# Second layer: 128 instead of 256 columns for the context's tiles in three projection blocks

## The chip, the cores and the metric

One Trainium2 chip, and of it one core. The metric is the time of one execution on the device in microseconds, as the median of several runs. The core's engines run side by side and meet by semaphores: TensorE multiplies (PE in the profile, and PEld for its loading of weights), VectorE (DVE) and ScalarE (ACT) work element by element, GpSimd (POOL) too, and SyncE (SP) starts most of the transfers from HBM.

## The reference, cut to what matters

Two layers of a block that mixes tokens and then runs a feed-forward part. There are 256 tokens of context and 256 of the sequence proper (x). Of the context the second layer, the last, needs only what the sequence reads from it: keys, values and the state of two scans. Its queries and its output gates have no reader.

```python
pc = split_cols(hc @ w_in + b_in)        # context, 256 tokens
px = split_cols(hx @ w_in + b_in)        # sequence, 256 tokens
mc, mx = mlstm_mixer(pc[0:6], px[0:6], ...)
gc, gx = hgrn2_mixer(pc[6:10], px[6:10], ...)
ac, ax = diff_mixer(pc[10:13], px[10:13], ...)
# with_ctx is False in the last layer: mc, gc and ac are not formed
# columns of w_in, in order: mLSTM q 384, k 384, v 384, output gate 384, i 8, f 8,
#   HGRN2 q 512, f 1024, v 256, gate 256, attention q 384, k 384, v 384
```

## The kernel before

All 512 tokens stand as four tiles of 128: tiles 0 and 1 are the context, 2 and 3 the sequence. The normalised input is kept transposed in `hT`, as two F32R parts: a rounded part, and what the rounding left. A weight block is fetched as F32 (`wraw`), ScalarE casts it to F32R (`whi`, line 297) and VectorE forms the rest (`wlo`, line 298). Each product is then made of three F32R matmuls: both parts of the activations by `whi` (`upper`), and the rounded part by `wlo` (`lower`). All of them are issued by one helper, `mm` in line 302, so that line stands for every projection of the kernel. No F32R matmul of the kernel has a moving operand of under 256 columns: they have 256, 400 or 512.

`gemm_tm` is the projection with tokens on the partitions of the output. The stationary operand (lhsT) is a 128x128 piece of `hT`, and the moving operand is the weight block, 256 columns wide in the blocks here. A block comes in two halves of the contraction with four pieces of 128 rows each. In each half, for each of the tiles in turn, `upper` issues eight matmuls; then `lower` issues four for each tile. Each matmul has a stationary piece of its own. Tiles 0 and 1 share a PSUM bank, and so do tiles 2 and 3; at the end `evac` takes each bank out with the bias added.

In the second layer (`l == 1`, `full` false) `qt` is (2, 3): blocks that hold queries or gates alone are computed for the sequence's two tiles only. The queries of the attention and of the mLSTM, however, are 384 columns wide, and so are the values. Cut into blocks of 256 columns, the middle one of each three is mixed:

- attention, `O_DAQ + 256`: columns 0 to 127 are queries, 128 to 255 are keys (into `qk`, by `add_bias`, line 913)
- mLSTM values and gates, `O_MLV + 256`: columns 0 to 127 are values, 128 to 255 are output gates (by `ev_vo`, lines 1069 to 1077)
- mLSTM queries and keys, `O_MLQ + 256`: columns 0 to 127 are queries, 128 to 255 are keys (into `mqk`, by `add_bias`)

These three blocks are computed with all 256 columns for all four tiles.

What runs where, and in what order, is not written out by hand. The program is written in order, each engine gets one fixed list of instructions, and the list is made by a planner that works with its own estimates of durations and with priorities: work marked `high_priority` (the casts in `wload`) goes ahead, and independent work is put where an engine would wait. So the blocks of the projections are found as filling between the steps of other stages: the attention's middle block between the steps of the HGRN2 scan (`hg_mix`, lines 798 to 880), the values' middle block between the steps of the attention (`da_tile`, lines 982 to 1003), and the mLSTM queries and keys one after another in a dense run. Other names in the rows are `Qd` and `Ck` (operands of the HGRN2 scan), `aT` and `Vda` (weights and values of the attention, plain F32) and `ls`, `lf` and `ct` (small plain-F32 products of the mLSTM's gates, lines 721 and 723, with 32 and 16 columns moving).

Of the kernel before, what the change touches and what calls it, by code (L numbers as in the profile page):

```python
# [15 lines left out]
ALU = mybir.AluOpType  # L16
# [15 lines left out]
O_MLQ, O_MLV, O_MLO, O_MLI = 0, 768, 1152, 1536  # L32
O_HGQ, O_HGF, O_HGV = 1552, 2064, 3088
O_DAQ, O_DAV = 3600, 4368
# [67 lines left out]
def dit_block(ctx: ExitStack, tc: tile.TileContext, x, c, ctx_in, c_ctx, w_ada, b_ada, g_pre_mix,  # L102
# [3 lines left out]
    V, S, G, PE, SY = nc.vector, nc.scalar, nc.gpsimd, nc.tensor, nc.sync  # L106
# [18 lines left out]
    def nm(s):  # L125
        uid[0] += 1
        return f"{s}_{uid[0]}"

    def pst(shape, mm=False):
        if mm:  # L130
            return psm.tile(shape, F32, tag="mm", name=nm("mm"))
        return psx.tile(shape, F32, tag="mx", name=nm("mx"))
# [126 lines left out]
    def ada_step():  # L259
        pace[0] += 1  # L260
        if pending and pace[0] % pace[1] == 0:
            try:
                next(pending[0])
            except StopIteration:
                pending.pop(0)
                ada_step_now()
# [14 lines left out]
    def wload(srcs, hold=None, eng=None):  # L281

        tot = sum(src.shape[1] for src in srcs)
        dims = [P, 4, 256] if tot <= 256 else [P, 2, 512]
        raw = wp.tile(dims, F32, tag="wraw", name=nm("wraw"), bufs=3)
        if hold is not None:
            hi, lo = hold
        else:
            hi = wp.tile(dims, F32R, tag="whi", name=nm("whi"), bufs=2)
            lo = wp.tile(dims, F32R, tag="wlo", name=nm("wlo"), bufs=2)  # L290
        n = 0
        for src in srcs:
            nk, w = src.shape[0] // P, src.shape[1]
            SY.dma_start(out=raw[:, :nk, n:n + w], in_=src.rearrange("(k p) n -> p k n", p=P))
            n += w
        with tc.high_priority(offset=AHEAD):
            S.copy(hi[:, :nk, :n], raw[:, :nk, :n])  # L297
            (eng or V).tensor_tensor(lo[:, :nk, :n], raw[:, :nk, :n], hi[:, :nk, :n], op=ALU.subtract)  # L298
        return hi, lo

    def mm(ps, lhs, rhs, first, last):
        PE.matmul(ps, lhsT=lhs, rhs=rhs, start=first, stop=last, skip_group_check=True)  # L302

    def upper(ps, blk, act, t, first):
        hi, _, ks = blk
        for kk, k in enumerate(ks):
            mm(ps, act(0, k, t), hi[:, kk], first and kk == 0, False)
            mm(ps, act(1, k, t), hi[:, kk], False, False)

    def lower(ps, blk, act, t, last):  # L310
        _, lo, ks = blk
        for kk, k in enumerate(ks):
            mm(ps, act(0, k, t), lo[:, kk], False, last and k == ks[-1])

    def blocks_of(srcs, holds=None):

        k0 = 0
        for si, pieces in enumerate(srcs):
            nk, n = pieces[0].shape[0] // P, sum(p.shape[-1] for p in pieces)
            hi, lo = wload(pieces, holds and holds[si])  # L320
            yield hi[:, :, :n], lo[:, :, :n], range(k0, k0 + nk)
            k0 += nk

    def gemm_tm(srcs, act, tiles, evac, pre=None):

        n = sum(p.shape[-1] for p in srcs[0])
        tiles = list(tiles)
        wide = n > 256  # L330
        bank = lambda t: t if wide else t // 2
        banks = {b: pst([P, 512] if wide else [P, 2, 256], mm=True) for b in sorted({bank(t) for t in tiles})}
        dst = lambda t: banks[t][:, :n] if wide else banks[bank(t)][:, t % 2, :n]
        new = lambda t: wide or t - 1 not in tiles or t % 2 == 0
        for si, blk in enumerate(blocks_of(srcs)):
            end = si == len(srcs) - 1
            if pre is not None and end:
                pre()
            if wide and end:
                for t in tiles:  # L340
                    upper(dst(t), blk, act, t, si == 0)
                    lower(dst(t), blk, act, t, True)
                    evac([t], dst(t))
            else:

                for t in tiles:
                    upper(dst(t), blk, act, t, si == 0 and new(t))
                for t in tiles:
                    lower(dst(t), blk, act, t, end)
            ada_step()  # L350
        if not wide:
            for tb, b in banks.items():
                tt = [t for t in tiles if bank(t) == tb]
                evac(tt, b[:, tt[0] % 2:tt[-1] % 2 + 1, :n])
# [39 lines left out]
    def w_src(w, c0, n):  # L394
        return [[w[kh * 512:(kh + 1) * 512, c0:c0 + n]] for kh in range(2)]
# [26 lines left out]
    hact = lambda i, k, t: hT[i][:, k, t * P:(t + 1) * P]  # L422
# [186 lines left out]
    for l in range(DEPTH):  # L609
        full = l == 0  # L610
        lam_init = 0.8 - 0.6 * math.exp(-0.3 * l)
        qt = (0, 1, 2, 3) if full else (2, 3)
# [79 lines left out]
        if l == 0:  # L692
            b0_load()
            for t in range(4):
                ev_first([t], acc0[t])
        else:
            srcs = first_src(l)
            gemm_tm(srcs, hact, (0, 1), ev_first, pre=b0_load)
            late_norm()
            gemm_tm(srcs, hact, (2, 3), ev_first)  # L700
# [194 lines left out]
        def ev_g(tt, ps):  # L895

            for i, t in enumerate(tt):
# [4 lines left out]
                V.tensor_mul(g_, g_, sg)  # L902
        hg_proj(1)
        gemm_tm(w_src(w_in[l], O_HGV + 256, 256), hact, qt, ev_g, pre=bg.load)
        lockstep(hg_mix(2), hg_mix(3))
        hg_out(2)
# [2 lines left out]
        hst.close()  # L909


        def add_bias(dst, w, nb, bb):
            return lambda tt, ps: V.tensor_tensor(dst[:, tt[0]:tt[-1] + 1, w:w + nb], ps[:, :, :nb],
                                                  bb.over(0, nb, len(tt)), op=ALU.add)

        qk = stg.tile([P, 4, 768], F32, tag="qk", name=nm("qk"))
        for i in range(3):
            bb = Bias([b_in[l, O_DAQ + i * 256:O_DAQ + (i + 1) * 256]])
            gemm_tm(w_src(w_in[l], O_DAQ + i * 256, 256), hact, qt if i == 0 else range(4), add_bias(qk, i * 256, 256, bb), pre=bb.load)
        bb = Bias([b_in[l, O_DAV:O_DAV + 256]])  # L920
        gemm_tm(w_src(w_in[l], O_DAV, 256), hact, range(4), add_bias(Vda, 0, 256, bb), pre=bb.load)

        wst = ExitStack()
# [135 lines left out]
        for i in range(3):  # L1059
            bb = Bias([b_in[l, O_MLV + i * 256:O_MLV + (i + 1) * 256]])  # L1060

            def ev_vo(tt, ps, i=i, bb=bb):
                c_ = 0
                while c_ < 256:
                    a = i * 256 + c_
                    if a < 384:
                        h, o = divmod(a, ML_D)
                        w = min(ML_D - o, 256 - c_, 384 - a)
                        V.tensor_tensor(Vml[:, tt[0]:tt[-1] + 1, h, o:o + w], ps[:, :, c_:c_ + w],
                                        bb.over(c_, c_ + w, len(tt)), op=ALU.add)  # L1070
                    else:
                        w = 256 - c_
                        for j, t in enumerate(tt):
                            if t in qt:
                                yv = Y[t][:, a - 384:a - 384 + w]
                                V.tensor_add(yv, ps[:, j, c_:], bb[:, c_:])
                                S.activation(yv, yv, AF.Sigmoid)
                    c_ += w
            gemm_tm(w_src(w_in[l], O_MLV + i * 256, 256), hact, range(4) if i < 2 else qt, ev_vo, pre=bb.load)
        mqk = stg.tile([P, 4, 768], F32, tag="qk", name=nm("mqk"))  # L1080
        for i in range(3):
            bb = Bias([b_in[l, O_MLQ + i * 256:O_MLQ + (i + 1) * 256]])
            gemm_tm(w_src(w_in[l], O_MLQ + i * 256, 256), hact, qt if i == 0 else range(4), add_bias(mqk, i * 256, 256, bb), pre=bb.load)

        dst_.close()
        gst = ExitStack()
# [165 lines left out]
        with tc.tile_pool(name=f"ff{l}", bufs=1, reuse_waits="tile") as ff:  # L1252
# [17 lines left out]
            for gi, (c0, ncb) in enumerate(groups):  # L1270
# [8 lines left out]
                for cp, a, b in blocks:  # L1279
                    cc_ = (c0 + 2 * cp) * P  # L1280
                    if cp not in GT:
                        GT[cp] = alloc()
                    n = b - a
# [91 lines left out]
```

## Time and profile before

| | us |
|---|---|
| median of 3 runs | 1347.56 |
| lowest and highest | 1346.56 and 1349.05 |
| the profiled execution, by the same clock | 1347.59 |
| its span, first to last instruction | 1345.9 |
| TensorE matmul busy | 1284.2 (95%) |
| TensorE weight load busy | 1094.6 (81%) |
| VectorE, ScalarE, GpSimd busy | 898.6, 624.9, 202.3 |
| mean granted TensorE clock, share of full speed | 0.985 |

The profile is one execution. A busy time is the union of an engine's instructions, and a matmul's length in it contains the way through the array, which the next matmul overlaps; so the pace of a run of matmuls is read from start to start and not from the length of one. A form such as `128*128 128x256` gives the stationary operand's size and then the moving operand's, and the names `mm<-whi,hT` put the moving operand before the stationary one. A row of the timeline joins successive instructions of one kind: start, time from the first start to the last end, and their count. A plain-F32 matmul stands in the records as two matmuls with two weight loads; an F32R matmul as one.

### The profile page before, as it was taken

To read this page: it belongs to the slowest core of one execution; us is meant where nothing else is said; L and a number is where in the kernel's file an instruction comes from. 1 tells how busy PE (TensorE), PEld (TensorE's weight loads), DVE (VectorE), ACT (ScalarE), POOL (GpSimd) and SP (SyncE) were. 2 spreads that over 40 slices of the span, in tenths; PEclk is the share of its full clock that TensorE was granted. 3 is DMA by queue.
4 is the path that set the end of the run, shared out by engine and by line. 5 is a ranking of instruction groups with operands and counts; after the bars stand their busy time and mean duration, and the time that the engine had idled before them with its cause. 6 is when DMAs were issued, how large, how long until landed. Compare 5 with 4: busy or idle time off the path is not lost.

```text
span 1345.9 us, 23128 instructions
## 1 busy us (share of the span) xinstructions
PE 1284.2 (95%) x9022; PEld 1094.6 (81%) x9022; DVE 898.6 (67%) x1564; ACT 624.9 (46%) x1188; POOL 202.3 (15%) x304
## 2 busy tenths in 40 slices
PE   7998999999989899999999999899999998999997
PEld 5785889778888798778887888778897998788886
DVE  4899998554688998476336348566855456666666
ACT  3436352578354653212221236546536724554543
POOL 3133202111142300001000003133111202000001
PEclk9999999999989999999999999899999999899999
DMA  9772526132244677477335235532331313456563
GB/s 290 227 221 75 164 64 201 41 114 72 95 141 142 192 253 229 141 255 243 116 100 178 94 111 151 148 95 63 104 95 51 122 47 109 142 188 188 188 188 125
DMA packets 158443, 194.05 MB, mean 144 GB/s; under 512 B 10524, under 2 KB 132806, under 8 KB 158334
## 3 DMA queue, kind: packets, MB, share of 16 engines
q1 hardware_dynamic: 156910, 188.89, 44.9%
q0 software_dynamic: 1424, 3.68, 1.0%
q8 instruction: 71, 1.16, 0.3%
q14 instruction: 38, 0.31, 0.1%
HBM read 191.47 MB, written 1.08 MB: 143 GB/s over the span
## 4 chain that ended last, share of the span: by engine, by line
PE 76%; DVE 10%; ACT 5%; issue 4%; DMA 3%; POOL 3%; SPq 0%; DVEq 0%; POOLq 0%; ACTq 0%
PE mm L302 62%; DMA araw<-in_w_ada_dram 2%; PE mx L1126 2%; DVE wlo L298 2%; PE mx L982 2%; PE mx L1003 1%; DVE acc L228 1%; PE mm L1114 1%; ACT whi L297 1%; POOL rstd L416 1%; PE mx L997 1%; PE mm L164 1%; DVE accq L228 1%; PE mx L880 1%; PE ada L233 1%
## 5 line engine op out<-in xcount | busy, mean ns | idle before, releaser
L297 ACT CAST whi<-wraw 128x1024 fp32r<-128x1024 f32 (+1 forms) x247 | 256.4, 1039 | 415.7 <-PE mm L302 365.2
L298 DVE TENSOR_TENSOR wlo<-wraw,whi 128x1024 fp32r<-128x1024 f32 (+1 forms) x243 | 295.8, 1218 | 193.0 <-PE mm L302 94.4
L302 PE MATMUL mm<-hT,whi 128*128 128x512 f32 (+1 forms) x1568 | 352.0, 372 | 4.4 <-ACT hT L465 2.1
L302 PEld LDWEIGHTS mm<-hT,whi 128*128 128x128 f32 x1568 | 270.8, 189 | 55.7 <-issue 4.0
L302 PE MATMUL mm<-whi,hT 128*128 128x256 f32 (+1 forms) x1792 | 264.3, 293 | 3.1 <-ACT hT L1157 1.4
L302 PEld LDWEIGHTS mm<-whi,hT 128*128 128x128 f32 x1792 | 234.0, 192 | 19.2 <-issue 8.4
L302 PE MATMUL mm<-hT,wlo 128*128 128x256 f32 (+1 forms) x960 | 185.0, 334 | 0.0
L302 PEld LDWEIGHTS mm<-hT,wlo 128*128 128x128 f32 x960 | 152.9, 190 | 21.1 <-issue 0.4
L302 PE MATMUL mm<-wlo,hT 128*128 128x256 f32 (+1 forms) x896 | 140.8, 292 | 0.0
L302 PE MATMUL mm<-whi,GT 128*128 128x512 f32 x504 | 129.5, 397 | 0.0
L302 PEld LDWEIGHTS mm<-wlo,hT 128*128 128x128 f32 x896 | 119.1, 191 | 10.9 <-issue 10.4
L302 PEld LDWEIGHTS mm<-whi,GT 128*128 128x128 f32 x504 | 93.7, 188 | 24.5 <-ACT whi L297 1.6
L228 DVE SCALAR_TENSOR_TENSOR accq<-araw,csil,accq 128x1024 f32<-128x1024 f32 x63 | 81.2, 1295 | 29.8 <-DMA araw<-in_w_ada_dram 29.7
L302 PE MATMUL mm<-wlo,GT 128*128 128x512 f32 x252 | 70.0, 396 | 0.0
L228 DVE SCALAR_TENSOR_TENSOR acc<-araw,csil,acc 128x1024 f32<-128x1024 f32 x49 | 62.8, 1306 | 4.6 <-DMA araw<-in_w_ada_dram 4.4
L302 PEld LDWEIGHTS mm<-wlo,GT 128*128 128x128 f32 x252 | 47.3, 188 | 11.3
L415 POOL TENSOR_SCALAR rstd<-hss 128x1 f32<-128x1 f32 (+2 forms) x44 | 18.8, 427 | 241.7 <-ACT hsq L656 159.9
L1327 POOL TENSOR_TENSOR Z<-Z,gg 128x512 f32<-128x512 f32 x6 | 9.4, 1572 | 234.1 <-ACT sqz L1326 234.1
L988 ACT ACTIVATE e<-mx,damx 128x512 f32<-128x512 f32 (+1 forms) x48 | 29.3, 618 | 26.3 <-DVE damx L985 26.3
L811 ACT COPY Ck<-Kh 128x512 f32<-128x512 f32 (+1 forms) x56 | 28.8, 525 | 25.7 <-DVE Kh L836 18.9
L416 POOL TENSOR_TENSOR rstd<-rstd,mhalf 128x1 f32<-128x1 f32 (+2 forms) x58 | 40.0, 690 | 4.7
L984 DVE TENSOR_REDUCE damx<-mx 128x1 f32<-128x512 f32 (+1 forms) x48 | 28.3, 598 | 18.0 <-PE mx L982 17.1
(283 smaller groups left out, 1499.9 us busy)
## 6 DMA issues: line engine op xcount, KB each, us to landing
araw<-in_w_ada_dram SPq DMA_DIRECT2D x80, 512.0 KB
wraw<-in_w_in_dram SPq DMA_DIRECT2D x68, 512.0 KB
wraw<-in_w_ffn_down_dram SPq DMA_DIRECT2D x50, 512.0 KB
wraw<-in_w_ffn_gate_dram SPq DMA_DIRECT2D x48, 512.0 KB
wraw<-in_w_ffn_up_dram SPq DMA_DIRECT2D x48, 512.0 KB
wraw<-in_w_out_dram SPq DMA_DIRECT2D x24, 512.0 KB
aw<-in_w_ada_dram SPq DMA_DIRECT2D x16, 512.0 KB
wraw<-in_w_in_dram SPq DMA_DIRECT2D x12, 256.0 KB
```

What stands on the lines that cost most here:

```text
L164: PE.matmul(acc0[3][:, :P], lhsT=ident, rhs=ident, start=True, stop=True, skip_group_check=True)
L228: V.scalar_tensor_tensor(out=a, in0=raw, scalar=csil[:, k, r:r + 1], in1=a, op0=ALU.mult, op1=ALU.add)
L297: S.copy(hi[:, :nk, :n], raw[:, :nk, :n])
L298: (eng or V).tensor_tensor(lo[:, :nk, :n], raw[:, :nk, :n], hi[:, :nk, :n], op=ALU.subtract)
L302: PE.matmul(ps, lhsT=lhs, rhs=rhs, start=first, stop=last, skip_group_check=True)
L415: G.tensor_scalar(o[:, :width], ss, 1.0 / n, EPS, ALU.mult, ALU.add)
L416: G.tensor_tensor(o[:, :width], o[:, :width], mhalf[:, :width], op=ALU.pow)
L811: S.copy(C[:, q0:].rearrange("p (a b i) -> p b a i", b=2, i=m), vap(K_, 2 * m * pq0, [[512 + m, 2], [2 * m, np_], [1, m]]))
L982: PE.matmul(pv[j], lhsT=qkT[0][64 * j:64 * j + DA_D, h, t * P:(t + 1) * P], rhs=qkT[1][64 * j:64 * j + DA_D, h, :nk], start=True, stop=True)
L984: V.reduce_max(mx[:, j:j + 1], pv[j], axis=AX.X)
L988: S.activation(e[:, j, :nk], pv[j], AF.Exp, bias=mx[:, 2 + j:3 + j], scale=sc, accum_out=mx[:, 4 + j:5 + j])
L1126: PE.matmul(po[:, i, d_, :], lhsT=W[d_, s_][0][:, t * P - W[d_, s_][2]:(t + 1) * P - W[d_, s_][2]], rhs=Vml[:, s_, h, :], start=n_ == 0, s ...
```

## The change

`gemm_tm` gets an argument `ctx_cols`. Where it is given, the matmuls of tiles 0 and 1 read only those columns of the weight block and write only those of the bank; tiles 2 and 3 are as before. `need` gives the pair of columns for the middle block (`i == 1`) in the second layer, and nothing elsewhere. `add_bias` evacuates only these columns of tiles 0 and 1. `ev_vo` is unchanged: it took no gates from tiles 0 and 1 of the second layer before either. The count of matmuls, the weight loads, the transfers and the casts are unchanged.

```diff
-    def gemm_tm(srcs, act, tiles, evac, pre=None):
+    def gemm_tm(srcs, act, tiles, evac, pre=None, ctx_cols=None):
...
+        part = lambda t: slice(*ctx_cols) if ctx_cols and t < 2 else slice(0, n)
...
+            of = lambda t: (blk[0][:, :, part(t)], blk[1][:, :, part(t)], blk[2])
...
                 for t in tiles:
-                    upper(dst(t), blk, act, t, si == 0 and new(t))
+                    upper(dst(t)[:, part(t)], of(t), act, t, si == 0 and new(t))
                 for t in tiles:
-                    lower(dst(t), blk, act, t, end)
+                    lower(dst(t)[:, part(t)], of(t), act, t, end)
...
-        def add_bias(dst, w, nb, bb):
-            return lambda tt, ps: V.tensor_tensor(dst[:, tt[0]:tt[-1] + 1, w:w + nb], ps[:, :, :nb],
-                                                  bb.over(0, nb, len(tt)), op=ALU.add)
+        need = lambda i, a, b: (a, b) if i == 1 and not full else None
+
+        def add_bias(dst, w, nb, bb, cc_=None):
+            def ev(tt, ps):
+                a, b = cc_ if cc_ and tt[0] < 2 else (0, nb)
+                V.tensor_tensor(dst[:, tt[0]:tt[-1] + 1, w + a:w + b], ps[:, :, a:b], bb.over(a, b, len(tt)), op=ALU.add)
+            return ev
...
-            gemm_tm(w_src(w_in[l], O_DAQ + i * 256, 256), hact, qt if i == 0 else range(4), add_bias(qk, i * 256, 256, bb), pre=bb.load)
+            gemm_tm(w_src(w_in[l], O_DAQ + i * 256, 256), hact, qt if i == 0 else range(4), add_bias(qk, i * 256, 256, bb, need(i, 128, 256)),
+                    pre=bb.load, ctx_cols=need(i, 128, 256))
...
-            gemm_tm(w_src(w_in[l], O_MLV + i * 256, 256), hact, range(4) if i < 2 else qt, ev_vo, pre=bb.load)
+            gemm_tm(w_src(w_in[l], O_MLV + i * 256, 256), hact, range(4) if i < 2 else qt, ev_vo, pre=bb.load, ctx_cols=need(i, 0, 128))
...
-            gemm_tm(w_src(w_in[l], O_MLQ + i * 256, 256), hact, qt if i == 0 else range(4), add_bias(mqk, i * 256, 256, bb), pre=bb.load)
+            gemm_tm(w_src(w_in[l], O_MLQ + i * 256, 256), hact, qt if i == 0 else range(4), add_bias(mqk, i * 256, 256, bb, need(i, 128, 256)),
+                    pre=bb.load, ctx_cols=need(i, 128, 256))
```

## Rows read from the trace of the kernel before

**Rows 1.** The page: span, and each engine's busy time.

```profile
span 1345.9 us, 23128 instructions
PE 1284.2 (95%) x9022; PEld 1094.6 (81%) x9022; DVE 898.6 (67%) x1564; ACT 624.9 (46%) x1188; POOL 202.3 (15%) x304
```

**Rows 2.** The page: the chain that ended last, by engine and by line.

```profile
PE 76%; DVE 10%; ACT 5%; issue 4%; DMA 3%; POOL 3%; SPq 0%; DVEq 0%; POOLq 0%; ACTq 0%
PE mm L302 62%; DMA araw<-in_w_ada_dram 2%; PE mx L1126 2%; DVE wlo L298 2%; PE mx L982 2%; PE mx L1003 1%; DVE acc L228 1%; PE mm L1114 1%; ACT whi L297 1%; POOL rstd L416 1%; PE mx L997 1%; PE mm L164 1%; DVE accq L228 1%; PE mx L880 1%; PE ada L233 1%
```

**Rows 3.** Busy time in the stretches of the three mixed blocks.

```profile
core 0: us, PE busy (x) PEld busy (x) DVE busy (x) ACT busy (x) POOL busy (x), PEclk, DMA share, GB/s
952.65:976.00 23.35, 22.76 (x278) 19.76 (x277) 18.09 (x53) 12.38 (x38) 0.13 (x1) 1.00 0.19 55
1023.90:1051.50 27.60, 26.51 (x169) 20.14 (x167) 15.74 (x40) 17.85 (x51) 4.91 (x14) 1.00 0.15 44
1066.03:1077.70 11.67, 11.67 (x100) 11.67 (x99) 3.76 (x4) 5.27 (x9) 2.15 (x3) 1.00 0.60 190
```

**Rows 4.** Timeline of PE through the third block: start, us, count.

```profile
1066.03 4.00 PE L302 MATMUL mm<-whi,hT 128*128 128x256 f32 x32
1069.87 2.08 PE L302 MATMUL mm<-wlo,hT 128*128 128x256 f32 x16
1071.79 4.00 PE L302 MATMUL mm<-whi,hT 128*128 128x256 f32 x32
1075.63 2.08 PE L302 MATMUL mm<-wlo,hT 128*128 128x256 f32 x16
```

**Rows 5.** Timeline of PE: 512-column, 256-column and 16-column matmuls, each with its successor.

```profile
868.40 3.79 PE L302 MATMUL mm<-hT,whi 128*128 128x512 f32 x16
872.03 1.98 PE L302 MATMUL mm<-hT,wlo 128*128 128x512 f32 x8
...
887.60 2.08 PE L302 MATMUL mm<-hT,whi 128*128 128x256 f32 x16
889.52 1.12 PE L302 MATMUL mm<-hT,wlo 128*128 128x256 f32 x8
...
890.62 0.60 PE L723 MATMUL mx<-lf,ct 128*128 128x16 f32 x4
891.06 3.22 PE L302 MATMUL mm<-hT,whi 128*128 128x512 f32 x13
```

**Rows 6.** Timeline of PE: 96-column plain-F32 matmuls of the attention, with their successor.

```profile
1018.35 1.97 PE L1003 MATMUL mx<-Vda,aT 128*128 128x96 f32 x16
1020.10 0.36 PE L1024 MATMUL mx<-Mp,ident 128*128 128x256 f32 x1
```

**Rows 7.** A matmul and weight loads by form: busy us, mean ns of one.

```profile
L1003 PE MATMUL mx<-Vda,aT 128*128 128x96 f32 x160 | 21.3, 275 | 0.0
...
L302 PEld LDWEIGHTS mm<-whi,hT 128*128 128x128 f32 x1792 | 234.0, 192 | 19.2 <-issue 8.4 <-ACT hT L1157 3.8 <-ACT hT L529 3.2
L723 PEld LDWEIGHTS mx<-lf,ct 128*128 128x128 f32 x8 | 1.1, 192 | 0.0
L820 PEld LDWEIGHTS mx<-Qd,Ck 128*32 128x32 f32 x192 | 2.3, 111 | 3.8 <-ACT Ck L811 2.9 <-issue 0.4
```

**Rows 8.** Timeline of PE: plain-F32 matmuls of 256 columns, two records each.

```profile
924.52 0.59 PE L866 MATMUL mx<-Qd,Kh 128*128 128x256 f32 x2
924.95 0.59 PE L867 MATMUL mx<-Qd,Kh 128*128 128x256 f32 x2
```

**Rows 9.** Evacuations into mqk on DVE: ns least/median/most, first and last start.

```profile
L913 DVE TENSOR_TENSOR mqk<-mm,brow x11: 670/691/693, 318.6 to 1090.5; 128x512 f32<-128x512 f32 x11
```

**Rows 10.** Timeline of DVE: an evacuation of 256 columns.

```profile
1060.20 0.42 DVE L1076 TENSOR_TENSOR Y<-mm,brow 128x256 f32<-128x256 f32 x1 [3.72 <-PE mm L302]
```

**Rows 11.** What PE waited for in the second stretch: us, times, longest.

```profile
PE mx L982 <- ACT e L988: 1.0, 1, 1.0
```

## The prediction

> **What bounds the kernel now.** I read the page first. TensorE is busy for 1284.2 of a span of 1345.9 us, and the weight loads alone for 1094.6 [rows 1]. The chain of waits says the same from the end backwards: 76% of it is TensorE and 62% the matmuls of line 302 [rows 2]. Then I read the windows of the three blocks that change. TensorE is busy for 22.76 of 23.35 us, 26.51 of 27.60 us and 11.67 of 11.67 us, at the full granted clock (1.00, that is 2.4 GHz) in all three, while VectorE and ScalarE have room [rows 3]. The timeline of the third block has 32, 16, 32 and 16 matmuls end to end [rows 4]; in the other two the same 96 matmuls fill the places between the steps of the scan and of the attention. So a microsecond of TensorE's pace, won or lost here, is nearly a microsecond of the kernel. The question is what one matmul paces at with 128 columns instead of 256.
>
> **The change part by part.** Per block there are 2 halves x 2 tiles of context x (8 upper + 4 lower) = 48 matmuls, in three blocks 144. Each still has its own 128x128 stationary piece; only the moving side halves.
>
> *What a matmul paces at now.* In the third block the second 32 start 1.92 us after the 16 before them, so 120 ns each [rows 4]. Elsewhere 16 of 256 columns take from 887.60 to 889.52, again 120 ns, and 16 of 512 columns from 868.40 to 872.03, 227 ns [rows 5]. The difference, 107 ns for 256 columns, is 0.418 ns a column, and 13 ns are left over per matmul. On that line 128 columns would pace at 120 - 53.5 = 66.5 ns.
>
> *What the weight load allows.* The load of a 128x128 piece doesn't shrink. Four matmuls of the mLSTM's gates move only 16 columns, with a fresh 128x128 piece each. They take from 890.62 to 891.06, 110 ns each [rows 5], where their own columns would explain a few ns. Sixteen records of 96 columns in the attention take from 1018.35 to 1020.10, 109 ns each; counted to the last end, less that one's own 275 ns [rows 7], it is (1.97 - 0.275)/15 = 113 ns [rows 6]. So two widths six times apart pace alike, at 109 to 113 ns. The loads' own lengths agree: 192 ns for 128 columns of weights, for F32R and for plain F32 alike, and 111 ns for 32 columns, which makes 0.84 ns a column and 108 ns for 128 columns [rows 7]. I take 112 ns as the floor per matmul with a fresh piece. The matmuls of 256 columns, at 120, stand only just above it: the load hides under 107 ns of streaming now, and under 53 ns it can't.
>
> The Trainium skill, TensorE: Matmul & The Clock Gate, section LDWEIGHTS, has a load take the stationary column count over 1.2 per ns, an estimate of 107 ns for 128 columns whatever the other operand. By that price alone the sum would be 144 x 13 = 1.9 us less. The trace's own rows give 3 to 6 ns more, and I keep these.
>
> *The sum.* 144 x (120 - 112) = 1.15 us less, 0.38 of it per block. No row shows an F32R matmul of 128 columns, so this is bounded from both sides. The best is the line through the wide ones: 144 x 53.5 = 7.7 us less. The worst is that a narrow F32R product takes what a plain-F32 one takes: that has two records with two loads, each at 0.43/2 us = 215 ns for 256 columns [rows 8]. At 128 columns each would stream in 107 and be held to 112 by its load, 224 ns in all: 144 x (224 - 120) = 15.0 us more. I take 112 because the nearest rows have the same stationary piece and moving operands narrower than its load. The 13 ns that F32R has left over at 256 and 512 might be paid on top of the load's 107 too. Then the pace is 120 and nothing is won: the near end of the likeliest case is 0.
>
> *The rest of it.* Two evacuations, of the attention's and the mLSTM's keys for the context, go from 0.69 us [rows 9] to about 0.42 [rows 10], 0.27 less each. VectorE is at 18.09 of 23.35 and 3.76 of 11.67 us there [rows 3] and the next blocks' matmuls run meanwhile, so I cost it at nothing; laid bare it would be 0.5 us at most. The values' evacuation is as before. Casts, transfers and bias rows are untouched, none is moved, and no wait is added. Weight blocks would be wanted 0.2 us sooner per half. Beside the four groups of the third block, casts of about a microsecond fill 5.27 of 11.67 us on ScalarE [rows 3], so that is covered.
>
> *The order.* The planner estimates a duration for the shorter matmuls, and the first two blocks are its filling. If its view of them changes, fillings move by some places. What can be won there is TensorE's idle time, 0.59 and 1.09 us [rows 3], whose largest piece is one wait of 1.0 us for the attention's exponential [rows 11]. If it were doubled, as much would be lost. So I allow 1.7 us either way, and take nothing.
>
> The sum goes against the profiled execution, 1347.59 us (span 1345.9 and 1.7 around it), which is the median of 1347.56 in all but name: 1347.59 - 1.15 = 1346.4 us. The likeliest case's own range is 1347.59 - 1.15 - 1.7 = 1344.7 to 1347.59 + 1.7 = 1349.3.
>
> **The rivals.**
>
> *Narrow F32R matmuls fall to the plain-F32 rate* (slower). The place is the 48 context matmuls of each block and the price 214 to 224 ns instead of 120; it decides against the change as soon as the pace is over 120, and visibly (2.7 us) from 139. For it: no F32R matmul of the kernel has fewer than 256 columns, so the trace has nothing below that to lean on, and 256 columns (107 ns) are just what one weight load takes (108), so a single-pass form that counts on this cover may lose its speed below it. Against it: between 256 and 512 F32R has one record per product and one straight line, and nothing hints at a step. Price: 144 x 94 to 104 = 13.5 to 15.0 us. TensorE's idle places in the second block could swallow 1.1 of it. Time: 1360.0 to 1362.6, middle 1361.3.
>
> *The load is hidden after all* (faster). Its place is the same, its mechanism that loads of successive pieces overlap each other and not only the matmul, so that the columns set the pace: 66.5 ns, 7.7 us less, 1339.9. For it: loads of 192 ns do overlap one another at a pace of 120. Against it: they do not at 16 and at 96 columns, where the wish would be the same. The Trainium skill, TensorE: Matmul & The Clock Gate, section Back-to-back issue gap, speaks for this case: it has 56 ns for isolated matmuls of 128 columns and about 81 ns sustained with their loads, and by the latter an estimate is 144 x 39 = 5.6 us less, 1342.0. The 109 to 113 ns of this trace, on loads of 4-byte weights, disagree.
>
> *The change doesn't do what it says* can be left out: the columns of both operands are cut in the code for exactly these matmuls, so their form must read 128x128 afterwards.
>
> **How the numbers follow.** Changes within 0.2%, 2.7 us, I call the same; that is about what a measurement of this kernel tells from nothing. The floor by weight loads has 0.54, the plain-F32 rate 0.31, the hidden load 0.15. The first lies within 2.7 us but for the far ends of the planner's 1.7 us (0.02 on either side); the second is slower altogether; the third is faster but for a remainder (0.14 and 0.01). That makes faster 0.16, same 0.51, slower 0.33. The range takes in the first two cases. Below it begins 1 us under the first's own range, as the runs shown spread by about that, at 1343.7; above it ends 1 us over the second's, at 1363.6. It leaves out the hidden load.
>
> **What would show it.** In the profile of the changed kernel line 302 has 144 matmuls of the form 128x128 and 144 fewer of 256 (less what records go missing), and one record each. The third block's groups tell the pace: the context's 16 upper ones in 1.8 us if the load is the floor, 3.4 to 3.6 us at the plain-F32 rate, 1.1 us if hidden, and the block from 11.67 to 11.3, 16.2 to 16.7, or 9.1 us. The weight loads of line 302 keep their 192 ns and become back to back there. Two evacuations fall to about 0.42 us. The prediction is wrong if the pace is not 109 to 120, and wrong in another way if the pace holds but the first two stretches change by more than 2 us through their order.

## The result, and the profile after

The changed kernel takes 1365.0 us (median of 4 runs, 1358.88 to 1368.62), the kernel before 1347.06 (4 runs, one more than in the table above, 1345.97 to 1349.05). The ratio is 1.0127, with a 95% interval of 1.0088 to 1.0166: slower, outside the forecast's range, and 18.6 us above its number. The profiled execution took 1364.77 us.

Three lines of the page. The span is 17.2 us longer, and TensorE's busy time 13.7 [rows 1].

```profile
span 1363.1 us, 23129 instructions
PE 1297.9 (95%) x9022; PEld 1107.0 (81%) x9022; DVE 899.2 (66%) x1564; ACT 623.8 (46%) x1186; POOL 201.5 (15%) x304
PEclk9999999999989999999999999999897899799999
```

The count of matmuls is as before, so the extra busy time is not more work. The last line is the granted TensorE clock in 40 slices: 8, 7, 8 and 7 stand in the 29th, 31st, 32nd and 35th slices.

Where does it arise? The second layer's scan of the second pair of heads starts at 943.3 us before and at 943.4 after. From that start to the mLSTM's transposes, which follow the last block of its queries and keys, it is 145.8 us before and 163.0 after: +17.2, the whole difference of the spans. These are the windows of that stretch, first of the kernel before, then of the changed one: start and end, length, busy time of PE, PEld, DVE, ACT and POOL with counts, granted clock, DMA share, GB/s.

```profile
943.30:1089.10 145.80, 142.69 (x1268) 127.09 (x1268) 86.83 (x189) 75.46 (x176) 23.90 (x48) 1.00 0.31 92
```

```profile
943.40:1106.40 163.00, 155.34 (x1268) 138.29 (x1268) 86.73 (x189) 73.25 (x174) 22.46 (x48) 0.91 0.28 82
```

Two things changed: TensorE's idle time went from 3.1 to 7.7 us, and the granted clock from 1.00 to 0.91. The three blocks' own windows in the changed kernel, to be held against [rows 3]:

```profile
952.70:983.38 30.68, 27.12 (x277) 23.50 (x276) 19.02 (x58) 13.66 (x39) 1.76 (x5) 0.83 0.15 42
1031.24:1068.84 37.60, 35.68 (x172) 28.57 (x172) 16.49 (x39) 19.77 (x55) 4.75 (x14) 0.73 0.11 32
1083.69:1094.98 11.29, 11.29 (x99) 11.29 (x99) 3.57 (x4) 3.16 (x3) 0.00 (x0) 1.00 0.50 154
```

The third block, a dense run, is 0.38 us shorter, at a clock of 1.00. The first two, which are filling between other steps, are 7.3 and 10.0 us longer, at 0.83 and 0.73.

The third block's timeline in the changed kernel, against [rows 4]. A row carries the form of its first matmul, so the 32 are 16 of 128 and 16 of 256 columns:

```profile
1083.74 3.87 PE L302 MATMUL mm<-whi,hT 128*128 128x128 f32 x32
1087.45 2.02 PE L302 MATMUL mm<-wlo,hT 128*128 128x128 f32 x16
1089.30 3.87 PE L302 MATMUL mm<-whi,hT 128*128 128x128 f32 x32
1093.01 2.02 PE L302 MATMUL mm<-wlo,hT 128*128 128x128 f32 x16
1094.86 1.36 PE L302 MATMUL mm<-whi,hT 128*128 128x256 f32 x10
```

From 1083.74 to 1087.45 are 3.71 us. Less 16 x 120 ns for the wide ones, 1.79 are left for 16 narrow ones: 112 ns each. The next 16 give (1.85 - 0.96)/8 = 111 ns.

Then the clock. Windows of the changed kernel's first two blocks, cut where the clock changes:

```profile
953.00:957.50 4.50, 2.97 (x64) 2.60 (x64) 4.50 (x13) 1.11 (x3) 0.00 (x0) 1.00 0.33 98
957.60:961.00 3.40, 3.40 (x44) 2.84 (x43) 2.80 (x10) 2.20 (x7) 0.00 (x0) 0.50 0.07 24
961.00:967.70 6.70, 4.70 (x78) 4.00 (x72) 4.58 (x12) 5.20 (x18) 0.00 (x0) 1.00 0.01 2
967.80:974.70 6.90, 6.90 (x31) 6.27 (x28) 5.10 (x19) 1.27 (x4) 0.00 (x0) 0.51 0.25 76
1032.80:1039.40 6.60, 6.60 (x32) 6.59 (x32) 3.48 (x11) 2.76 (x7) 0.00 (x0) 0.50 0.38 99
1046.30:1053.10 6.80, 6.80 (x30) 6.19 (x30) 3.17 (x8) 4.22 (x10) 0.59 (x2) 0.50 0.00 0
1060.10:1066.70 6.60, 6.60 (x24) 4.95 (x24) 2.37 (x6) 2.30 (x7) 0.00 (x0) 0.50 0.01 2
```

Five pieces run at 0.50, that is at 1.2 GHz. By the trace's record of the clock they are 30.7 us in all (the windows are cut a little inside them); before, no piece of this stretch does. Ahead of the first drop TensorE was busy for 2.97 of 4.50 us. In such a piece everything on TensorE is slow, the narrow matmuls and their neighbours alike. The timeline of the changed kernel there:

```profile
1031.29 0.34 PE L302 MATMUL mm<-whi,hT 128*128 128x128 f32 x2
1031.70 1.18 PE L990 MATMUL mx<-qkT,qkT 48*128 48x512 f32 x2
1032.81 2.82 PE L302 MATMUL mm<-whi,hT 128*128 128x128 f32 x12
1035.43 1.07 PE L1005 MATMUL mx<-ident,e 128*128 128x128 f32 x4
```

Twelve narrow matmuls take 2.62 us from start to next start, 218 ns each, and the four transposes behind them 1.07 where the same four took 0.60 before.

This drop, the first of the second stretch, doesn't come behind a run of narrow matmuls. The two in the first row above are the only ones in the 16.6 us ahead of it, and TensorE was busy there nearly as it was before: for 15.94 of 16.60 us (1015.9 to 1032.5), where the same steps of the kernel before (1008.5 to 1025.1) have 16.00 of 16.60. There the clock stayed at 1.00.

Last, the idle time. Timeline of PE in the scan, before and then after; brackets give the wait ahead of a row:

```profile
953.27 0.33 PE L823 MATMUL mx<-Qd,Ck 128*32 128x32 f32 x16 [0.34 <-ACT Ck L811]
953.53 1.92 PE L302 MATMUL mm<-whi,hT 128*128 128x256 f32 x14
955.42 0.33 PE L823 MATMUL mx<-Qd,Ck 128*32 128x32 f32 x16
955.68 1.34 PE L302 MATMUL mm<-whi,hT 128*128 128x256 f32 x9
956.95 0.33 PE L823 MATMUL mx<-Qd,Ck 128*32 128x32 f32 x16
```

```profile
953.35 0.33 PE L825 MATMUL mx<-Qd,Ck 128*32 128x32 f32 x16 [0.38 <-ACT Ck L813]
953.61 1.00 PE L302 MATMUL mm<-whi,hT 128*128 128x128 f32 x7
955.49 0.33 PE L825 MATMUL mx<-Qd,Ck 128*32 128x32 f32 x16 [0.88 <-DVE Qd L841]
955.75 0.78 PE L302 MATMUL mm<-whi,hT 128*128 128x128 f32 x5
956.83 0.33 PE L825 MATMUL mx<-Qd,Ck 128*32 128x32 f32 x16 [0.30 <-DVE T L845]
957.09 1.25 PE L302 MATMUL mm<-whi,hT 128*128 128x128 f32 x6
```

Between two steps of the scan stood 14 projection matmuls and then 9; now 7 and 5 do, though each is barely shorter. They run out before the step's operand is there, and TensorE waits 0.88 us. What was not placed is done later: by the same timeline the projection matmuls in a row behind the scan are 224 instead of 193, and those behind the attention 276 instead of 227, 80 more in the two dense runs.

### The profile page after: what moved, and what is told of

It reads as the page before. It is cut to its first block, busy times and chain, and to the rows that moved or that the text cites. A ratio compares the mean times of both kernels' runs of the same rounds, so it can differ in the third digit from the quotient of the medians.

```text
span 1363.1 us, 23129 instructions
## 1 busy us (share of the span) xinstructions
PE 1297.9 (95%) x9022; PEld 1107.0 (81%) x9022; DVE 899.2 (66%) x1564; ACT 623.8 (46%) x1186; POOL 201.5 (15%) x304
## 4 chain that ended last, share of the span: by engine, by line
PE 74%; DVE 10%; ACT 5%; issue 4%; POOL 3%; DMA 3%; SPq 0%; DVEq 0%; POOLq 0%; ACTq 0%
PE mm L302 60%; DMA araw<-in_w_ada_dram 2%; DVE wlo L298 2%; PE mx L1135 2%; PE mx L990 2%; PE mx L1011 1%; DVE Qd L841 1%; ACT whi L297 1%; POOL rstd L418 1%; PE mx L1005 1%; PE mm L1123 1%; PE mm L164 1%; DVE accq L228 1%; PE mx L882 1%; PE ada L233 1%
## 5 line engine op out<-in xcount | busy, mean ns | idle before, releaser
L302 PE MATMUL mm<-whi,hT 128*128 128x256 f32 (+2 forms) x1792 | 271.1, 298 | 3.0 <-ACT hT L1166 1.4
L302 PEld LDWEIGHTS mm<-whi,hT 128*128 128x128 f32 x1792 | 240.3, 197 | 21.9 <-issue 11.1
L302 PEld LDWEIGHTS mm<-hT,wlo 128*128 128x128 f32 x960 | 153.1, 191 | 21.1 <-issue 0.4
L302 PE MATMUL mm<-wlo,hT 128*128 128x256 f32 (+2 forms) x896 | 140.3, 293 | 0.0
L990 PE MATMUL mx<-qkT,qkT 48*128 48x512 f32 (+1 forms) x96 | 36.6, 579 | 4.2 <-ACT e L996 3.7
```

Source lines behind the costliest of these rows:

```text
L990: PE.matmul(pv[j], lhsT=qkT[0][64 * j:64 * j + DA_D, h, t * P:(t + 1) * P], rhs=qkT[1][64 * j:64 * j + DA_D, h, :nk], start=True, stop=True)
```

## The experiments

The theory after these rows had two parts: the planner's new order loses time even at the full clock, and narrow matmuls in its thin gaps lose the clock. The rivals: the clock alone, brought down by narrow matmuls wherever they stand, with the order as bystander; or the order alone.

**Order and width apart.** Two kernels cross them. A helper fixes the order in which each engine issues what is in the stretch; it adds no wait. One kernel has the narrow matmuls in the order of before, the other has the kernel before in the order of after. (Lines below 302 move down in them: 302 is 393.)

```diff
+def set_order(tc, nc):                 # ISSUE: the other kernel's order, one list per engine
+    by = {i.name: i for i in nc.cur_bb.bb.instructions}
+    for seq in ISSUE:
+        for a, b in zip(seq, seq[1:]):
+            tc.add_manual_dep(by[f"I-{b}"], f"I-{a}",
+                              mybir.DependencyInfo(mybir.DependencyClass.NoSync, mybir.DependencyReason.DATA), reason="order")
...
+        set_order(tc, nc)
```

*Narrow matmuls, old order.*

> The changed kernel, with each engine's instructions issued in the order that they had before the change. Theory order: the planner put about half as many of the narrow matmuls in each gap of the scan and of the attention (7, 5, 6 where before 14, 9, 8), TensorE ran dry there and its granted clock fell; with the old order back the clock stays at 2.4 GHz in both stretches and the time is 1.2 us under the kernel before, 1344 to 1348. Theory columns: the narrow matmuls themselves, which pace at 112 ns and stream for 53 of them, let the clock fall; with the old order it still falls in both stretches and the time stays 5 to 18 us over the kernel before, 1352 to 1366. Pace at the full clock 110 to 113 ns by both.

Measured: 1346.61 us against 1347.01, ratio 1.0009 (0.9995 to 1.0022): no difference. The stretch, and the one piece of it at half clock:

```profile
944.50:1090.40 145.90, 142.60 (x1267) 127.62 (x1267) 86.20 (x189) 75.63 (x176) 23.94 (x48) 0.99 0.31 92
1040.60:1044.00 3.40, 3.40 (x18) 3.40 (x18) 1.46 (x4) 2.19 (x6) 0.74 (x2) 0.51 0.34 119
```

*Wide matmuls, new order.*

> The kernel before, all 256 columns, with each engine's instructions issued in the order that they have in the changed kernel. Theory order: half as many fillings per gap leave TensorE idle as in the changed kernel, the clock falls in both stretches, 1355 to 1366. Theory columns: the wide matmuls keep the clock up, and the other order alone costs what idle it makes, 0 to 3 us: 1346 to 1351.

Measured: 1355.81 against 1347.01, ratio 1.0068 (1.0049 to 1.0088). The stretch, and from what TensorE waited for in it the three largest and the counterpart of the 0.88 us above (us, times, longest):

```profile
944.70:1098.70 154.00, 144.42 (x1268) 127.32 (x1267) 87.11 (x189) 72.79 (x174) 22.44 (x48) 1.00 0.29 87
```

```profile
PE mx L1088 <- DVE e L1085: 3.1, 4, 1.3
PE mx L911 <- ACT Ck L902: 1.8, 2, 1.3
PE mx L1073 <- ACT e L1079: 1.6, 2, 1.1
PE mx L914 <- DVE Qd L930: 0.8, 1, 0.8
```

So the order alone, with the very matmuls of before, costs 8.2 us of this stretch: 6.5 more idle time, and 1.7 more busy time. The clock is 1.00. That refutes the clock as the only cause. Neither theory came out whole: the time lies at the low end of what the theory of the order gave, but the fall of the clock that it forecast is missing. Narrow matmuls in this same order take 163.0 us, 9.0 more, and only they have the half clock. And narrow matmuls in the old order stand at half clock for 3.4 us only, so width alone isn't the cause of most of it either. It takes both.

These traces are of one execution each. The mean granted clock over the whole program, which is known of every execution, bears them out: 0.983 to 0.991 before (19 runs, mean 0.987), 0.984 to 0.987 with wide matmuls in the new order (4, mean 0.986), 0.981 to 0.989 with narrow ones in the old order (10, mean 0.984), 0.972 to 0.979 with both (4, mean 0.974). So the new order alone leaves the clock, and the width alone costs a little of it.

**One block at a time.** Each of three kernels narrows one block and undoes the change for the other two (here a part of that edit):

```diff
-                    pre=bb.load, ctx_cols=need(i, 128, 256))
+                    pre=bb.load, ctx_cols=None)
```

> Narrow columns in the first block alone (attention's queries and keys, between the steps of the scan). In the changed kernel the stretch from the scan's start to the attention's first transposes took 62.9 us against 55.6, and with wide products in the same order 59.4: 3.8 by the order and 3.5 by the clock. If the stretches add up (second alone was 10.4 over): 4 to 8 us over the kernel before, 1351 to 1355, TensorE's clock down for 3 to 11 us between 943 and 980. If the loss needs both blocks, within 2 us.

> Narrow columns in the second block alone (values and gates, between the steps of the attention). In the changed kernel the clock was down for 20.4 us in that stretch, in three pieces. If each stretch brings its own loss, whatever the reason, about 8 to 11 us more than before: 1355 to 1358; the first block's stretch (943 to 977 us) has the full clock. If the loss needs both blocks, within 2 us of before.

> Narrow columns in the third block alone (mLSTM queries and keys), which runs dense. Both theories: 48 matmuls at 112 instead of 120 ns, no fall of the clock between 1060 and 1090 us, 0.4 us less, 1346 to 1348, which can't be told from no change. If the clock falls here too, 2 to 4 us more.

| narrowed | us | before | ratio (95%) | the stretch, us | half clock in it, us |
|---|---|---|---|---|---|
| first block only | 1353.2 | 1346.67 | 1.0050 (1.0037 to 1.0063) | 153.1 | 10.2 |
| second only | 1357.41 | 1347.01 | 1.0078 (1.0048 to 1.0109) | 159.8 | 30.7 |
| third only | 1347.96 | 1347.01 | 1.0000 (0.9988 to 1.0012) | 145.4 | none |

The two fillings carry the whole loss: 6.5 and 10.4 us of the medians, 16.9 together against 17.9 for the full change. How much of it the clock has differs between executions of one kernel with one order: the four of the second block only go from 1352.0 us at a mean clock of 0.987 to 1360.3 at 0.976. The fastest, with the clock of before, is still 5 us over. The block in the dense run wins 0.4 in its stretch (145.8 to 145.4), too little for the medians to show.

**Does a dense run of narrow matmuls lose the clock?** In the kernel before, each matmul of the third block was made as two of 128 columns, 192 in a row:

```diff
+                halves_ = (slice(0, 128), slice(128, 256)) if split else (slice(0, n),)
...
-                    upper(dst(t), blk, act, t, si == 0 and new(t))
+                    for c in halves_:
+                        upper(dst(t)[:, c], cut(c), act, t, si == 0 and new(t) and c.start == 0)
...
```

> The kernel before; in the third block (mLSTM queries and keys, dense, no gaps) each of the 96 matmuls of 256 columns is made as two of 128 with a weight load each: 192 narrow ones in a row. At 112 ns the block takes 21.5 us instead of 11.7, 9.8 us more: 1356 to 1358. If narrow products alone let the clock fall, with no idle beside them, they pace at 213 ns for part of it and it is 12 to 25 us more: 1359 to 1372. If weights of the same piece twice running were loaded once or overlapped, under 5 us more.

Measured: 1356.62 against 1347.18, ratio 1.0064 (1.0048 to 1.0081). The block's window and its timeline:

```profile
1065.50:1086.89 21.39, 21.39 (x195) 21.39 (x193) 3.76 (x4) 5.27 (x9) 2.16 (x3) 1.00 0.33 103
```

```profile
1065.50 7.26 PE L302 MATMUL mm<-whi,hT 128*128 128x128 f32 x64
1072.60 3.74 PE L302 MATMUL mm<-wlo,hT 128*128 128x128 f32 x32
```

64 in 7.10 us are 111 ns each, and the clock stays at 1.00 for all 21.4 us. So in a dense run neither the narrow form nor its pace lowered the clock. The cost, 9.7 us in the block, is the doubled count at an unreduced weight load.

**192 columns instead of 128.** If fewer matmuls stand in a gap because each moves fewer columns, 192 columns would get more places than 128. If the planner takes a higher price for a column below 256, 192 would get as many or fewer.

```diff
-add_bias(qk, i * 256, 256, bb, need(i, 128, 256)),
-                    pre=bb.load, ctx_cols=need(i, 128, 256))
+add_bias(qk, i * 256, 256, bb, need(i, 64, 256)),
+                    pre=bb.load, ctx_cols=need(i, 64, 256))
```

> The changed kernel with 192 instead of 128 columns for the context's tiles (64 columns more than are used), planner's own order. In the planned order the scan's gaps now hold 5, 3, 3, 3 products where the changed kernel has 7, 5, 6, 8 and the kernel before 14, 9, 9, 10. Theory planner (it prices a product of under 256 columns far too high, the more columns the worse; the thin gaps leave TensorE idle): idle of TensorE between the scan's start and the mLSTM transposes 9 to 13 us (before 3.1), time 9 to 16 us over the kernel before, 1356 to 1363, at least as slow as the order of the changed kernel with wide products (1356). Theory columns (the loss comes from too little streaming per product): half way between 128 and 256, idle 4 to 6 us, 4 to 9 us over, 1351 to 1356. Pace by both 109 to 113 ns, as the weight load sets it (192 columns would stream in 93).

Measured: 1365.17 against 1347.18, ratio 1.0135 (1.012 to 1.015), with 27.3 us at half clock. TensorE is idle for 9.5 us of the stretch, as the theory of the planner had it, but the time lies 2.2 us above its range, which had no fall of the clock in it. The timeline in the scan:

```profile
954.30 0.81 PE L302 MATMUL mm<-whi,hT 128*128 128x192 f32 x5
956.18 0.33 PE L825 MATMUL mx<-Qd,Ck 128*32 128x32 f32 x16 [1.07 <-DVE Qd L841]
```

The places by the programs' own order, projection matmuls in each gap of the scan from the start of the stretch:

```
before             4 3 22 12 3 5 14 9 9 10 7 17 8 5 5 5 1
after              4 3 22 12 3 5  7 5 6  8 7 11 1 5 6 3 1
192 columns        4 3 22 12 3 5  5 3 3  3 6 12 4 0 2 2 1
```

Where the first block's context tiles begin (7th to 10th gap) the counts fall from 14, 9, 9, 10 to 7, 5, 6, 8 at 128 columns and to 5, 3, 3, 3 at 192. At 192 all four gaps hold narrow matmuls alone, about a third of the places; at 128 the first two do, about half, while of the next 6 three are wide and the 8 are all wide. That is as if the planner took a column below 256 for four times its price, 512 and 768 instead of 256. The measured pace is 112 ns for 128 columns against 120 for 256. The price itself was not read, only what it did to the order.

**Narrow and wide alternating.** The same narrow matmuls, but with the tiles in the innermost loop, so that context and sequence take turns and a gap holds some of both.

```diff
+            elif ctx_cols:
+                for kk, k in enumerate(ks):
+                    for j in range(2):
+                        for t in tiles:
+                            mm(dst(t)[:, part(t)], act(j, k, t), hi[:, kk, part(t)], ...)
```

> The changed kernel with the tiles in the innermost loop, so that narrow and wide matmuls alternate by twos instead of sixteen narrow ones and sixteen wide ones; planner's own order, whose gaps hold 9, 7, 5, 7 (before 14, 9, 9, 10; changed 7, 5, 6, 8). Theory order plus columns (thin gaps cost 8 us by idle; narrow products in thin gaps let the clock fall, 9 us more): the gaps are as thin, so 6 to 9 us remain, but each gap streams more and the clock falls for less than half of the 30.8 us: 1353 to 1360. If the clock falls by the thin gaps alone whatever fills them: 1361 to 1367.

Measured: 1358.26 against 1347.18, ratio 1.0077 (1.0062 to 1.0092). The four gaps hold 9, 7, 5 and 7 matmuls. The stretch:

```profile
942.50:1098.10 155.60, 146.30 (x1268) 130.66 (x1267) 86.83 (x189) 72.79 (x174) 23.45 (x48) 0.97 0.29 86
```

TensorE is idle for 9.3 us of it, near the 9.6 with wide matmuls in the new order, and it is 7.4 shorter than after, with 10.2 us at half clock instead of 30.7. But this execution took 1354.55 us, the fastest of the four by 3.7, at a mean clock of 0.986 where the others have 0.978 to 0.982; the changed kernel has 0.972 to 0.979. So mixing keeps part of the clock and leaves the idle time. The planner's order differs here too, so this run doesn't separate the mixing from the order.

**The same work saved without narrow matmuls.** Queries, keys, values and gates are 384 columns wide. Cut into blocks of 384, no block is mixed, and nothing has under 256 columns. First for the attention's queries and keys and all four of the mLSTM:

```diff
-        for i in range(3):
+        for i in range(2 if not full else 0):
+            bb = Bias([b_in[l, O_MLQ + i * 384:O_MLQ + (i + 1) * 384]], bp)
+            gemm_tm(w384(O_MLQ + i * 384), hact, qt if i == 0 else range(4), add384(mqk, i * 384, bb), pre=bb.load)
+        for i in range(3 if full else 0):
...
```

A block of over 256 columns takes the other branch of `gemm_tm`: a PSUM bank for each tile, so four for a block of all tiles, and an eviction for each.

> The kernel before with the second layer's projections cut at the columns' own borders: queries, keys, values and gates of the mLSTM, and queries and keys of the attention, as blocks of 384 columns, so that the context computes only what is used and no product is narrow. At 160 + 13 = 173 ns a product of 384 columns: context 34.6 to 24.9 us, sequence 51.8 to 49.8, together 11.7 us less of TensorE. If TensorE stays the bound: 7 to 12 us less, 1335 to 1340. Rival: the scan and the attention have less filling per gap and one block holds all four accumulator banks, so idle or a fall of the clock eats it: 1342 to 1352.

Measured: 1348.88 against 1347.18, ratio 1.0016 (1.0006 to 1.0026). The stretch and its largest wait:

```profile
944.40:1093.20 148.80, 137.00 (x980) 117.85 (x979) 87.76 (x189) 73.72 (x179) 22.64 (x48) 0.94 0.31 91
```

```profile
PE mm L302 <- DVE qk L923: 5.0, 1, 5.0
```

TensorE is busy 5.7 us less than before, but idle 8.7 more, 5.0 of it in one wait for an eviction of the attention's queries and keys, and 17 us stand at half clock. This execution, 1351.59 us, is one of the slowest of ten (1346.53 to 1351.96), yet the mean clock of all ten, 0.976 to 0.984, is at or under the least of before (0.984). So as filling the saving is lost to idle time and to the clock; what the order, the eviction and the banks have of it no run separates. The last kernel does it in the dense run alone, for the mLSTM's queries and keys:

> The kernel before with the mLSTM's queries and keys of the second layer, and these alone, cut as two blocks of 384 columns (queries for the sequence's tiles, keys for all four) instead of three of 256; they run dense, and the planned order of the scan and of the attention stays that of the kernel before. Context: 96 products of 256 columns at 120 ns become 48 of 384 at 173 ns per tile pair and block (11.5 to 8.3 us), sequence 17.3 to 16.6: 3.9 us less, 1342.5 to 1344.5, clock in that stretch at 2.4 GHz. Rival: four banks held by one block make TensorE wait for an evacuation, as it did for 5.0 us once with all blocks at 384; then 1345 to 1349.

Measured: 1340.86 against 1346.67, ratio 0.9960 (0.9949 to 0.9972), faster than the kernel before and the changed one, and 1.6 us under the expected range. The stretch and the timeline in the run:

```profile
942.40:1084.40 142.00, 138.94 (x1171) 123.17 (x1171) 87.12 (x192) 74.88 (x178) 22.68 (x47) 1.00 0.31 90
```

```profile
1067.76 2.93 PE L302 MATMUL mm<-whi,hT 128*128 128x384 f32 x16
1070.53 1.55 PE L302 MATMUL mm<-wlo,hT 128*128 128x384 f32 x8
```

Sixteen in 2.77 us are 173 ns each. The queries and keys were 10 tile-blocks of 24 matmuls at 120 ns, 28.8 us; now they are 6 of 24 at 173 ns, 24.9. The stretch is 3.8 us shorter, as this sum has it. The rest of the 5.8 us between the medians lies elsewhere in the program, where the two profiles differ in the pieces at half clock (42.2 us in all before, 32.4 here); no run explains it.

## Why the prediction was wrong, point by point

**What bounds the kernel: right.** What TensorE lost, idle or in the clock, the kernel lost: +17.2 us in the stretch and in the span.

**The pace: right.** Forecast 112 ns, measured 111 to 112 in the third block and in the split one. One record for each matmul, as forecast (144 of them; the means, 327 and 288 ns, hold the pieces at half clock too):

```profile
L302 PE MATMUL mm<-whi,hT 128*128 128x128 f32 x96 | 17.5, 327 | 0.0
L302 PE MATMUL mm<-wlo,hT 128*128 128x128 f32 x48 | 7.1, 288 | 0.0
```

The third block gave its 0.38 us (11.67 to 11.29). With the old order kept, the whole change takes 145.9 us of the stretch, with 3.4 at half clock. Those cost at most 1.7, so at the full clock it would be between 144.2 and 145.9. The sum's 144.65 lies inside. The medians don't show the gain: 1.15 us would be a ratio of 0.9991, just under the interval's 0.9995 to 1.0022, and the mean clock of these ten runs, 0.9839 against 0.9865 before, can cost up to 3.5 us of 1347.

**The evictions: right.** On VectorE, the one of 256 columns into the attention's queries and keys is the least of its group (ns least, median, most); that into the mLSTM's is 425:

```profile
L920 DVE TENSOR_TENSOR qk<-mm,brow x11: 422/687/691, 196.5 to 996.3; 128x512 f32<-128x512 f32 x10, 128x256 f32<-128x256 f32 x1
```

**The order: this step failed.** The prediction wrote: "If its view of them changes, fillings move by some places. What can be won there is TensorE's idle time, 0.59 and 1.09 us ... If it were doubled, as much would be lost. So I allow 1.7 us either way, and take nothing." Measured with the wide matmuls, it is 8.2 us. The bound was taken from the idle time of before. That limits what a better order can win, and says nothing on what a worse one loses: a gap with too little filling is idle for as long as the other engines need, and the matmuls left over run later with no gap to hide in. Its size is near that of the filling which left the gaps: the 80 more matmuls in the dense runs are 9.6 us at 120 ns. (A slip beside it: the 0.02 that the likeliest case gives to slower doesn't follow from its own range, whose upper end, 1.7 us, lies within the 2.7.)

**The clock: an unstated step, and it failed too.** The sum took 1.00 in all three stretches because the rows of before show it. In the new order the narrow matmuls stand at 0.50 for 30.7 us, and the stretch is 9.0 us longer than with wide ones. The three facts are measured apart: 9.6 us of idle time in small places with wide matmuls, clock 1.00; 21.4 us of narrow matmuls without a gap, 1.00; both together, 0.50 in five pieces. Why the combination does it, the runs don't show. It is not simply narrow matmuls in the gap just ahead: the drop at 1032.6 us has two of them in the 16.6 us before it. Executions of one kernel differ too, so the moment at which the pauses come may have a part; that was not tested. The Trainium skill, TensorE: Matmul & The Clock Gate, section A second HAM failure mode: psum-queue depth-cycling, tells of a kernel in which TensorE pauses so often and briefly between groups of matmuls that its clock swings between the two levels. Here small pauses alone (wide matmuls in the new order) did not do it; with narrow matmuls in the same order they did.

**The rivals: both refuted as mechanisms.** At the plain-F32 rate the pace would be 214 to 224 ns at the full clock. The trace has 218 ns, but only where the clock is 0.50, and the transposes beside it double too. The time, 1365.0, is near that rival's 1361.3 by coincidence. The hidden load's 66.5 ns is seen nowhere, nor the 81 ns that the Trainium skill, TensorE: Matmul & The Clock Gate, section Back-to-back issue gap, has for this width: at the full clock 111 to 112 stand against it.

The prediction's own test had named it: the pace holds, and the first two stretches change by far more than 2 us. By the order alone, with wide matmuls, the stage of the scan is 3.8 us longer (59.40 against 55.60), that of the attention 1.0 (60.40 against 59.40), and the dense run behind them, which gets what they didn't place, 3.4 (34.20 against 30.80).

## What to carry to other kernels

Where a planner places work by its own estimates, changing an operation's shape changes its price, and so the place of everything around it: read the changed program's order (how many fillings stand in each gap) before you add up paces. Count the clock with it: it fell where the order had left TensorE small pauses and the matmuls were narrower. TensorE's idle time bounds what a better order can win; for what a worse one can lose, look at the filling that stands in the gaps. To spare columns of a mixed block, cut the blocks so that no block is mixed rather than narrow the matmuls below their weight load, and begin where the run is dense: 3.8 us less in that stretch there, and nothing won as filling.

## What was not expected of the hardware

- F32R matmuls of 128 columns keep one record and 111 to 112 ns, only 8 ns under those of 256: with a fresh 128x128 stationary piece each, half the columns save 7% of the time.
- The granted clock fell to 0.50 in five pieces, 30.7 us in all, with narrow matmuls in the new order, and stayed at 1.00 with wide ones in the same order, though TensorE was idle for more of that stretch (9.6 us against 7.7). One drop came with two narrow matmuls in the 16.6 us ahead of it. It also drags the neighbours down: the four transposes of 0.60 us took 1.07.
- How long the clock is down differs between executions of one program: with the second block alone narrowed, 1352.0 us at a mean clock of 0.987 and 1360.3 at 0.976.
